# Block products of the up projection: weight sums made by accumulating transfers, and 17 block tiles instead of 12 in the first network

## The chip, the cores and the metric

One core of one Trainium2 chip runs the kernel. The metric is device time of one execution in microseconds (us), the median of several runs. The core has a matrix engine (PE; its weight loads are shown as PEld), a vector engine (VectorE, DVE in the profile), an activation engine (ScalarE, ACT), a general engine (GpSimd, POOL) and an engine that mostly issues transfers (SyncE, SP). Each engine works through a queue of its own in order, and waits on semaphores for what other engines or transfers have to finish first.

## The reference: what is computed

Two residual layers over 512 tokens of width 1024, everything in float32. Each layer has a token mixer (first a state-space mixer, "s5", then forgetting attention, "fox") and a gated feed-forward network with a short convolution. Only the networks are touched here:

```
def conv_ffn(h, w_up, conv_w, conv_b, w_down):
    up = h @ w_up                       # (512, 1024) @ (1024, 5632)
    a, b = jnp.split(up, 2, axis=-1)    # two branches of 2816 columns
    ...
    a_conv = conv_b
    for i in range(CONV_W):             # causal, width 3
        a_conv = a_conv + ap[:, i:i + S] * conv_w[i]
    return (jax.nn.silu(a_conv) * b) @ w_down
```

## The kernel before, in words

**Precision.** Every float32 matrix is split in two float32r parts, `hi` (a rounded copy, made by ScalarE, L287) and `lo` (the rest, value minus `hi`, made by VectorE, L288). A product of two matrices is three matrix multiplies: hi·hi, hi·lo and lo·hi. This splitting is `put_parts`, L285. Weights arrive as float32 in tiles called `raw` (three buffers, L191), are split into a ring of five `w_hi` tiles and five `w_lo` tiles (L272 to L283, L195), and only then reach PE.

**Stages.** `build` (L1504) runs s5, the first network (`ffn`, L597, with l = 0), fox, and the second network (l = 1). A network has 22 column tiles f of 128 columns in each branch. The weights of tile f are two `raw` tiles of 512 KB, number 2f for the convolved branch and 2f + 1 for the other. The 22 tiles are worked in four groups of 6, 5, 6 and 5 (`GROUPS`); while a later group is made, the down projection of the group before is worked off in pieces between its tiles (`down`, L672), 18 or 15 matrix multiplies of 512 columns for each of 8 output tiles. `gated` (L614) does convolution, silu, the product of the branches and the split of the result.

**Two ways to make a tile.** A tile in `WHOLE_TILES` (L49) goes through `product` (L308, with `apart=True`): two weight tiles, two halves of 256 tokens, 8 blocks of the inner dimension and three parts, so 96 matrix multiplies of 256 columns, from L304. Any other tile goes through `quarters` (L529), which treats the two weight tiles as a 2 by 2 block matrix (rows: a = tile 2f, b = tile 2f + 1; columns: the two halves of the inner dimension) and the tokens likewise, and forms the product with seven block products instead of eight, Winograd's form of Strassen's scheme: 7 × 4 × 3 = 84 matrix multiplies of 256 columns, from L566. It needs four sums of weight quarters, which VectorE makes in the tiles `sums` (L548, L549, L551, L552; they all go through the helper of L537 and carry its number in the profile):

- s1 = a21 + a22, s2 = s1 − a11, s3 = a11 − a21, s4 = a12 − s2

and four sums of the tokens, made once for each network by `forms_x` (L490). The quarters a11, a12, s1, s2, s4, s3 and a22 are then split in that order of writing; a22 goes into a tile of its own, `e`, with one buffer. PE takes them in the order a11, s1, a12, s2, s4, a22, s3 (L579 to L592), 12 matrix multiplies each. Three of the products pile up on others in PSUM: s2 on a11, s4 on s1, s3 on both of a11 and s2. In between ScalarE has to copy the earlier sum out (`copy`, L571 and L573), and VectorE adds the copies into the result (L584, L588, L593, L594).

**What sets the order.** The kernel is written for a framework that traces the program and, at build time, places each instruction in the queue of its engine by its place in the program and by when it expects operands and buffers to be ready; `issue_after` adds an order by hand. The queues are fixed when the kernel runs. The first network also works off the modulation vectors of later sub-layers in the background (`ada_units`, L248: one VectorE instruction on 128x1024 elements with a transfer of 512 KB; two for each tile from f = 6 on, `SUMS`, L50).

**Before the change** the first network makes tiles 0 to 4, 8, 11, 14, 17 and 20 whole and the other 12 by blocks; the second makes tiles 0 to 3 whole and 18 by blocks. No transfer is issued from GpSimd.

Of the kernel before, what the change touches and what calls it, by code (L numbers as in the profile page):

```python
# [45 lines left out]
ROWS_FROM = 0  # L46
GROUPS = (6, 5, 6, 5)
TAIL = 4
WHOLE_TILES = (0, 1, 2, 3, 4, 8, 11, 14, 17, 20), (0, 1, 2, 3)  # L49
SUMS = (0,) * 6 + (2,) * 16  # L50
FIRST = (("c", (KT,)), ("s5_prm", (3, G // 2)))
REST = (
# [11 lines left out]
class Trunk:  # L64
# [425 lines left out]
    def forms_x(self, pool, x, b):  # L490
# [10 lines left out]
                yield  # L501
        self.tx = {}

        def form(n, u, v):
            t = pool.tile([P, H, N], F32, name="sums", bufs=2)
            nc.vector.tensor_tensor(t, u, v, ALU.subtract)
# [12 lines left out]

        f1 = form(1, b[0][:, :, t2], b[0][:, :, t1])  # L520
        yield
        f2 = form(2, b[1][:, :, t2], f1)
        yield
        form(4, f2, b[1][:, :, t1])
        yield
        form(3, b[1][:, :, t2], b[0][:, :, t2])
        yield

    def quarters(self, pool, l, f, x, finish):  # L529

        nc = self.nc
        H, N = KT // 2, S // 2
        t1, t2 = HALVES
        a, b = (self.raw([P, KT, P], self.io["w_up"][l][2 * f + j]) for j in range(2))
        a11, a12, a21, a22 = a[:, :H], a[:, H:], b[:, :H], b[:, H:]
        c, d = (pool.tile([P, 2, H, P], F32, name="sums", bufs=2) for _ in range(2))
        sub = lambda o, u, v, op=ALU.subtract: nc.vector.tensor_tensor(o, u, v, op)  # L537
# [12 lines left out]
        parts(c.rearrange("p n k m -> p (n k) m"), ("s1", "s2"))  # L550
        sub(d[:, 1], a11, a21)  # L551
        sub(d[:, 0], a12, c[:, 1])  # L552
        parts(d.rearrange("p n k m -> p (n k) m"), ("s4", "s3"))
        e = self.e or [pool.tile([P, H, P], F32R, name=n, tag="e" + n, bufs=1) for n in ("w_hi", "w_lo")]
        self.e = None
        parts(a22, ("a22",), e)
        quarter = lambda k, t: tuple(v[:, k * H:(k + 1) * H, t] for v in x)
        xs = {"b11": quarter(0, t1), "b21": quarter(1, t1), "b22": quarter(1, t2)}
        for n, v in self.tx.items():
# [8 lines left out]
                        skip_group_check=True,  # L568
                    )

        def copy(o):  # L571
            t = self.tmp.tile([P, N], F32, name="nm_h", bufs=4)
            nc.scalar.activation(t, o, AF.Copy)  # L573
            return t

        p1, p5 = (self.mm.tile([P, S], F32, name="mmp")[:, :N] for _ in range(2))
# [14 lines left out]
        c4 = copy(p4)  # L591
# [104 lines left out]
class Ew:  # L696
# [29 lines left out]
    def sub(self, a, b, out=None):  # L726
        return self.tt(a, b, ALU.subtract, out)
# [875 lines left out]
```

## Time and profile before

| | |
|---|---|
| median of 3 runs | 1193.79 us (1190.88 to 1197.5) |
| the profiled execution | 1197.65 us, of which the span from first to last instruction is 1195.9 us |
| PE busy | 1174.1 us, 98% |
| VectorE busy | 988.7 us, 83% |
| ScalarE busy | 592.4 us, 50% |
| GpSimd busy | 62.6 us, 5% |
| granted TensorE clock, mean | 0.991 |
| block tiles of the first network, with the down projection between | from 310 to 564 us |
| block tiles of the second network, likewise | from 891 to 1148 us |

A row of the groups reads: line, engine, operation, output<-inputs, shape, count | busy us, mean ns of one | idle time of the engine just before them, and what ended it. In a timeline the columns are start in us, length in us, engine, line, operation, tiles, and in square brackets the idle time before it and what ended it; SPq is SyncE's queue that issues transfers, and its lengths include waiting for a free buffer. PE's matrix multiplies are pipelined: one lasts longer than the distance to the next, so their pace is read from the starts.

### The profile page before, as it was taken

How to read it: one execution, taken by the hardware profiler on the slowest of the kernel's cores; microseconds unless marked ns; L12 is line 12 of the kernel's file. 1: busy time of each engine (PE TensorE's matmuls, PEld its weight loads, DVE VectorE, ACT ScalarE, POOL GpSimd, SP SyncE). 2: the span in 40 equal slices, each digit the busy share in tenths (PEclk: the TensorE clock that was granted, in tenths of full speed). 3: DMA queues.
4: the chain of work that ended last, by engine and by line, in shares of the span. 5: the costliest groups of instructions: out<-in, count | busy, mean ns of one | idle time of the engine just before them, and what ended most of it. 6: DMA issues, size and time to landing. Idle time of an engine off the chain costs nothing.

```text
span 1195.9 us, 21116 instructions
## 1 busy us (share of the span) xinstructions
PE 1174.1 (98%) x8243; PEld 1026.5 (86%) x8243; DVE 988.7 (83%) x1824; ACT 592.4 (50%) x1069; POOL 62.6 (5%) x114
## 2 busy tenths in 40 slices
PE   7999999999999999999999999999999999999997
PEld 2455687899999999999899788878999999999987
DVE  8899977889888888887776788866899888888855
ACT  2554525346544454453453566554466555555543
POOL 1000000000000000000000443330000000000000
PEclk9999989999999999999999999999999999999999
DMA  9687758822264455554514655523123342343331
GB/s 359 226 256 251 230 167 303 295 92 89 87 204 131 159 174 170 185 184 139 194 36 138 209 185 166 200 76 97 47 75 96 124 124 86 111 124 95 104 88 72
DMA packets 73234, 183.83 MB, mean 154 GB/s; under 512 B 23231, under 2 KB 25503, under 8 KB 72111
## 3 DMA queue, kind: packets, MB, share of 16 engines
q1 hardware_dynamic: 72847, 181.96, 46.6%
q8 instruction: 65, 1.06, 0.4%
q10 hardware_dynamic: 288, 0.52, 0.1%
q14 instruction: 34, 0.28, 0.1%
HBM read 175.53 MB, written 6.92 MB: 153 GB/s over the span
## 4 chain that ended last, share of the span: by engine, by line
PE 86%; DVE 7%; DMA 3%; ACT 2%; issue 1%; POOL 0%; SPq 0%; DVEq 0%; ACTq 0%; POOLq 0%
PE mmp L304 42%; PE mmp L566 15%; PE aux L566 6%; PE mmp L1167 4%; PE mmp L1344 3%; PE mmp L1197 2%; DVE w_lo L288 2%; PE aux L1490 2%; PE aux L1473 1%; PE aux L1061 1%; PE aux L1053 1%; PE mmp L221 1%; PE aux L1443 1%; ACT w_hi L287 1%; DMA raw<-in_w_down 1%
## 5 line engine op out<-in xcount | busy, mean ns | idle before, releaser
L287 ACT ACTIVATE w_hi<-raw 128x1024 fp32r<-128x1024 f32 (+4 forms) x197 | 176.0, 900 | 146.9 <-PE mmp L304 75.5
L288 DVE TENSOR_TENSOR w_lo<-raw,w_hi 128x1024 fp32r<-128x1024 f32 (+4 forms) x197 | 203.4, 1036 | 29.7 <-ACT w_hi L287 25.2
L304 PE MATMUL mmp<-a_hi,w_hi 128*128 128x256 f32 (+1 forms) x600 | 185.9, 311 | 0.0
L304 PE MATMUL mmp<-a_hi,w_lo 128*128 128x256 f32 (+1 forms) x600 | 182.8, 306 | 0.0
L304 PE MATMUL mmp<-a_lo,w_hi 128*128 128x256 f32 (+1 forms) x600 | 182.7, 305 | 0.0
L304 PE MATMUL mmp<-ghi,w_hi 128*128 128x512 f32 (+1 forms) x392 | 143.9, 367 | 0.0
L304 PE MATMUL mmp<-glo,w_hi 128*128 128x512 f32 (+1 forms) x392 | 143.9, 367 | 0.0
L304 PE MATMUL mmp<-ghi,w_lo 128*128 128x512 f32 (+1 forms) x392 | 143.6, 366 | 0.0
L304 PEld LDWEIGHTS mmp<-a_hi,w_hi 128*128 128x128 f32 x600 | 112.4, 188 | 7.6 <-issue 2.6
L304 PEld LDWEIGHTS mmp<-a_hi,w_lo 128*128 128x128 f32 x600 | 112.5, 188 | 6.4
L304 PEld LDWEIGHTS mmp<-a_lo,w_hi 128*128 128x128 f32 x600 | 112.6, 188 | 4.8
L287 ACT ACTIVATE w_hi<-sums 128x1024 fp32r<-128x1024 f32 x68 | 71.6, 1060 | 65.9 <-DVE sums L537 27.4
L566 PE MATMUL mmp<-w_hi 128*128 128x256 f32 x360 | 99.6, 277 | 0.0
L566 PE MATMUL mmp<-w_hi,w_lo 128*128 128x256 f32 x360 | 99.5, 276 | 0.0
L566 PE MATMUL mmp<-w_lo,w_hi 128*128 128x256 f32 x360 | 99.4, 276 | 0.0
L288 DVE TENSOR_TENSOR w_lo<-sums,w_hi 128x1024 fp32r<-128x1024 f32 x68 | 82.4, 1220 | 7.6 <-ACT w_hi L287 6.5
L256 DVE CUSTOM_DVE_ANT_0 ada_raw<-ada_raw,ada_c,rest 128x1024 f32<-128x1024 f32 x64 | 83.7, 1326 | 5.1 <-DMA ada_raw<-in_ada_rows 5.1
L304 PEld LDWEIGHTS mmp<-ghi,w_lo 128*128 128x128 f32 x392 | 73.6, 188 | 12.3
L304 PEld LDWEIGHTS mmp<-ghi,w_hi 128*128 128x128 f32 x392 | 73.6, 188 | 11.2
L304 PEld LDWEIGHTS mmp<-glo,w_hi 128*128 128x128 f32 x392 | 73.6, 188 | 11.1
L378 DVE SCALAR_TENSOR_TENSOR h<-mmp,par,h 128x512 f32<-128x512 f32 (+1 forms) x98 | 62.9, 649 | 23.4 <-PE mmp L304 23.3
L566 PEld LDWEIGHTS mmp<-w_hi 128*128 128x128 f32 x360 | 67.6, 188 | 0.1
(317 smaller groups left out, 2833.0 us busy)
## 6 DMA issues: line engine op xcount, KB each, us to landing
raw<-in_w_up SPq DMA_DIRECT2D x88, 512.0 KB, 3.4
ada_raw<-in_ada_rows SPq DMA_DIRECT2D x64, 512.0 KB, 4.2
raw<-in_ada_w SPq DMA_DIRECT2D x32, 512.0 KB, 5.5
raw<-in_w_down SPq DMA_DIRECT2D x32, 384.0 KB, 3.2
raw<-in_w_down SPq DMA_DIRECT2D x32, 320.0 KB, 3.1
nf<-nfd SPq DMA_DIRECT2D x8, 1152.0 KB, 5.7
raw<-in_fox_qk SPq DMA_DIRECT2D x16, 512.0 KB, 3.2
h<-in_x SPq DMA_DIRECT2D x8, 512.0 KB, 5.5
```

The source lines that it names most:

```text
L221: self.last_mm = nc.tensor.matmul(ps[32 * qq:32 * qq + 32, :], self.sc32[:, k, :], w[:, q * S:(q + 1) * S], start=(step is steps[0]), stop ...
L256: nc.vector.tensor_tensor_reduce(w, w, self.crow, 1.0, self.ada_b[:, i, m:m + 1], ALU.mult, ALU.add, self.par[i][:, m:m + 1])
L287: nc.scalar.activation(hi, src, AF.Copy)
L288: self.late = (nc.vector.tensor_tensor(lo, src, hi.bitcast(F32), ALU.subtract).ins,)
L304: self.last_mm = self.nc.tensor.matmul(o, wt, xt[:, cols], start=(k == 0 and n == 0), stop=(k == nk - 1 and n == 2),)
L378: self.nc.vector.scalar_tensor_tensor(h, v, self.par[i][:, 16 + m:17 + m], h, op0=ALU.mult, op1=ALU.add,).ins,
L566: self.last_mm = nc.tensor.matmul(o, wt[:, k], xt[:, k], start=(first and k == 0 and n == 0), stop=(k == H - 1 and n == 2), skip_group_che ...
L1053: nc.tensor.matmul(yp[g2][:, k, :], t[:, 2 * k + g2], u[:, g, :], start=(k == 0), stop=False, skip_group_check=True,)
L1167: nc.tensor.matmul(ps, w[m][:, k, :], x[:, k], start=(k == 0), stop=(k == KT - 1))
L1197: nc.tensor.matmul(gps[m], wt, xt[:, k], start=(k == 0 and part == 0 and xt is yhi), stop=(k == KT - 1 and part == 1))
L1344: self.last_mm = nc.tensor.matmul(ps[q, b][:, :n], xt[:, k, tb], wt, start=(k == 0 and i == 0), stop=(k == KT - 1 and i == 2),)
L1490: nc.tensor.matmul(pv[:, c * P:], self.v[:, hp, k, r].rearrange("p t d -> p (t d)"), pp[:, r, c + 3 * k:NB + 3 * k, :].rearrange("p b t -> ...
```

## The change: sums by accumulating transfers, and fewer whole tiles

The four VectorE instructions for the weight sums are dropped. In their place come two ScalarE instructions that write negated copies, −a11 into a new tile `s2` (128x512, one buffer) and −a11, −a12 into `d` (128x1024, two buffers), and four transfers of 256 KB issued from GpSimd that add their source to what stands at the destination. `src` is the second weight tile in HBM:

1. a22 from HBM onto a21 in the raw tile `b`, which becomes s1;
2. a21 from HBM onto −a11 in `d`, which becomes −s3;
3. s1 from `b` onto −a11 in `s2`, which becomes s2;
4. s2 from `s2` onto −a12 in `d`, which becomes −s4.

The third needs the first, the fourth the third. The signs of t1, t3, s3 and s4 are turned, so that nothing else has to be negated but one copy out of PSUM. The split order is now (a11, a12), (s1, a22), (s2), (s3, s4), with s2 instead of a22 in the tile `e`. All this holds for all block tiles of both networks. In the first network tiles 8, 11, 14, 17 and 20 become block tiles.

```
-WHOLE_TILES = (0, 1, 2, 3, 4, 8, 11, 14, 17, 20), (0, 1, 2, 3)
+WHOLE_TILES = (0, 1, 2, 3, 4), (0, 1, 2, 3)
...
-        f1 = form(1, b[0][:, :, t2], b[0][:, :, t1])
+        f1 = form(1, b[0][:, :, t1], b[0][:, :, t2])
-        f2 = form(2, b[1][:, :, t2], f1)
+        f2 = form(2, b[1][:, :, t2], f1, ALU.add)
-        form(3, b[1][:, :, t2], b[0][:, :, t2])
+        form(3, b[0][:, :, t2], b[1][:, :, t2])
...
+        src = self.io["w_up"][l][2 * f + 1]
-        c, d = (pool.tile([P, 2, H, P], F32, name="sums", bufs=2) for _ in range(2))
+        d = pool.tile([P, 2, H, P], F32, name="sums", bufs=2)
+        s2 = pool.tile([P, H, P], F32, name="sum2", bufs=1)
+        plus = lambda o, u: nc.gpsimd.dma_start(o, u, accum_op=ALU.add)
...
+        plus(b[:, :H], src[:, H:])
+        nc.scalar.activation(s2, a[:, :H], AF.Copy, scale=-1.0)
+        nc.scalar.activation(d.rearrange("p n k m -> p (n k) m"), a, AF.Copy, scale=-1.0)
         parts(a, ("a11", "a12"))
-        sub(c[:, 0], a21, a22, ALU.add)
-        sub(c[:, 1], c[:, 0], a11)
-        parts(c.rearrange("p n k m -> p (n k) m"), ("s1", "s2"))
-        sub(d[:, 1], a11, a21)
-        sub(d[:, 0], a12, c[:, 1])
-        parts(d.rearrange("p n k m -> p (n k) m"), ("s4", "s3"))
+        plus(d[:, 0], src[:, :H])
+        plus(s2, b[:, :H])
+        parts(b, ("s1", "a22"))
+        plus(d[:, 1], s2)
         e = self.e or [pool.tile([P, H, P], F32R, name=n, tag="e" + n, bufs=1) for n in ("w_hi", "w_lo")]
-        parts(a22, ("a22",), e)
+        parts(s2, ("s2",), e)
+        parts(d.rearrange("p n k m -> p (n k) m"), ("s3", "s4"))
...
-        c5 = copy(p5)
+        c5 = copy(p5, -1.0)
...
-        sub(oa[:, t2], p5, c2, ALU.add)
+        sub(oa[:, t2], c2, p5)
```

More of the change, by code (lines that the diff above doesn't have):

```diff
@@ L502, in forms_x, with form @@
         self.tx = {}
-        def form(n, u, v):
+        def form(n, u, v, op=ALU.subtract):
             t = pool.tile([P, H, N], F32, name="sums", bufs=2)
-            nc.vector.tensor_tensor(t, u, v, ALU.subtract)
+            nc.vector.tensor_tensor(t, u, v, op)
             if n == 1:
@@ L533, in quarters @@
         t1, t2 = HALVES
+        src = self.io["w_up"][l][2 * f + 1]
         a, b = (self.raw([P, KT, P], self.io["w_up"][l][2 * f + j]) for j in range(2))
-        a11, a12, a21, a22 = a[:, :H], a[:, H:], b[:, :H], b[:, H:]
-        c, d = (pool.tile([P, 2, H, P], F32, name="sums", bufs=2) for _ in range(2))
+        d = pool.tile([P, 2, H, P], F32, name="sums", bufs=2)
+        s2 = pool.tile([P, H, P], F32, name="sum2", bufs=1)
         sub = lambda o, u, v, op=ALU.subtract: nc.vector.tensor_tensor(o, u, v, op)
+        plus = lambda o, u: nc.gpsimd.dma_start(o, u, accum_op=ALU.add)
         w = {}
@@ L569, in times, with copy @@
                     )
-        def copy(o):
+        def copy(o, scale=1.0):
             t = self.tmp.tile([P, N], F32, name="nm_h", bufs=4)
-            nc.scalar.activation(t, o, AF.Copy)
+            nc.scalar.activation(t, o, AF.Copy, scale=scale)
             return t
```

## The prediction

> **What bounds the kernel now.** I read the page's head first, then its chain of waits.
>
> ```profile
> span 1195.9 us, 21116 instructions
> PE 1174.1 (98%) x8243; PEld 1026.5 (86%) x8243; DVE 988.7 (83%) x1824; ACT 592.4 (50%) x1069; POOL 62.6 (5%) x114
> PE 86%; DVE 7%; DMA 3%; ACT 2%; issue 1%; POOL 0%; SPq 0%; DVEq 0%; ACTq 0%; POOLq 0%
> ```
>
> PE is both the busiest engine and 86% of the chain that ends last. An average hides stages, so the next view is the stretches in which block tiles are made: the first network, the first 44 us of block tiles in the second, and the rest of the second. The columns after the stretch are its length and each engine's busy time, then the granted clock, the DMA share and GB/s.
>
> ```profile
> 310.30:564.00 253.70, 253.70 (x1863) 238.99 (x1862) 216.20 (x320) 119.38 (x178) 0.52 (x1) 1.00 0.51 165
> 890.90:935.00 44.10, 43.81 (x360) 42.64 (x359) 42.55 (x64) 26.75 (x45) 0.00 (x0) 1.00 0.36 120
> 935.00:1148.40 213.40, 213.40 (x1528) 199.53 (x1527) 179.86 (x267) 113.75 (x177) 0.00 (x0) 1.00 0.35 107
> ```
>
> PE has no hole in the first and the third, and 0.3 us in the second, at full clock. VectorE is close behind: 85%, 96% and 84%. So in these stages time is gained only by giving PE fewer matrix multiplies, and lost wherever a weight or a freed PSUM bank comes later than PE asks for it. GpSimd does next to nothing there.
>
> **What the five exchanged tiles save.** The pace of PE is read from where a tile of each kind begins and where the work behind it begins: a whole tile first, then a block tile.
>
> ```profile
> 351.20 0.28 PE L304 MATMUL mmp<-a_hi,w_hi 128*128 128x256 f32 x1
> 362.11 0.39 PE L304 MATMUL mmp<-ghi,w_hi 128*128 128x512 f32 x1
> ...
> 366.21 0.28 PE L566 MATMUL mmp<-a_hi,w_hi 128*128 128x256 f32 x1
> 375.76 0.39 PE L304 MATMUL mmp<-ghi,w_hi 128*128 128x512 f32 x1
> ```
>
> A whole tile takes 362.11 − 351.20 = 10.91 us for 96 matrix multiplies, a block tile 375.76 − 366.21 = 9.55 us for 84; both go at 0.1137 us each, so neither waits for anything. The difference is 1.36 us, and five tiles make **6.8 us**. This is the whole gain in sight: the other 30 block tiles keep their 84 multiplies.
>
> **What moves between VectorE and ScalarE.** The groups by form give the prices.
>
> ```profile
> L288 DVE TENSOR_TENSOR w_lo<-raw,w_hi 128x1024 fp32r<-128x1024 f32 x100 | 123.8, 1242 | 21.6 <-ACT w_hi L287 17.2 <-PE aux L1344 3.7
> L288 DVE TENSOR_TENSOR w_lo<-sums,w_hi 128x1024 fp32r<-128x1024 f32 x68 | 82.4, 1220 | 7.6 <-ACT w_hi L287 6.5
> L287 ACT ACTIVATE w_hi<-sums 128x1024 fp32r<-128x1024 f32 x68 | 71.6, 1060 | 65.9 <-DVE sums L537 27.4 <-PE mmp L304 22.5 <-PE aux L566 5.7
> L537 DVE TENSOR_TENSOR sums<-raw 128x512 f32<-128x512 f32 x60 | 39.3, 687 | 20.9 <-DMA raw<-in_w_up 20.8
> L537 DVE TENSOR_TENSOR nm_t<-mmp,nm_h 128x256 f32<-128x256 f32 x90 | 35.3, 418 | 0.0
> L573 ACT ACTIVATE nm_h<-mmp 128x256 f32<-128x256 f32 x90 | 33.8, 377 | 42.1 <-PE mmp L566 42.1
> L288 DVE TENSOR_TENSOR w_lo<-raw,w_hi 128x512 fp32r<-128x512 f32 x30 | 20.5, 685 | 0.0
> L287 ACT ACTIVATE w_hi<-raw 128x512 fp32r<-128x512 f32 x30 | 18.7, 622 | 6.9 <-DMA raw<-in_w_up 6.8
> ```
>
> Each block tile loses four sums of 0.687 us on VectorE: 2.75 us, 33 us for the 12 old tiles of the first network and 49 us for the 18 of the second. Each exchanged tile gains on VectorE 3 × 1.22 + 0.685 − 2 × 1.242 = 1.86 us of splitting and four additions at 0.418, together 3.53 us, 17.7 us for five. VectorE in the first network goes from 216.2 to 216.2 − 33 + 17.7 = 201 us, of a stretch of 253.7 − 6.8 = 246.9, or 81%; in the second from 42.55 + 179.86 = 222.4 to 173 of 44.1 + 213.4 = 257.5, or 67%. As PE did not wait for VectorE before, none of this shortens anything; it is what makes room for the five tiles.
>
> ScalarE takes two negations a tile. No row shows one; the nearest are its copies of 128x512 and 128x1024, 0.622 + 1.060 = 1.68 us, and I take that. Over 17 tiles that is 28.6 us; the exchanged tiles add 5 × (3 × 1.060 + 0.622 − 2 × 1.06 + 4 × 0.377) = 16 us. ScalarE reaches 119.4 + 44.6 = 164 of 246.9 us, 66%, and about the same in the second network. Under PE's cover both cost nothing; the cover is gone only where an engine's order of work stands still, which is the rest of this text. The turned signs and the scaled copy keep their instructions and their prices.
>
> **What the transfers cost.** The trace has no transfer issued from GpSimd and none that adds. The nearest rows are other queues' transfers (size, then median us from issue to landing).
>
> ```profile
> raw<-in_w_up SPq DMA_DIRECT2D x88, 512.0 KB, 3.4
> nf<-nfd SPq DMA_DIRECT2D x8, 1152.0 KB, 5.7
> yt<-s_yd SPq DMA_DIRECT2D x16, 256.0 KB, 4.8
> s_ud<-uf SPq DMA_DIRECT2D x8, 256.0 KB, 3.1
> nfd<-nf_rows SPq DMA_DIRECT2D x1, 16.0 KB, 1.5
> ```
>
> The ends are 1.5 us (almost no bytes) and 5.7 us (over four times the bytes). The same size takes 3.1 and 4.8, and I take their middle, **4.0 us** each. The Trainium skill ("DMA: Bandwidth & Descriptors", the section on the anatomy of one SWDGE DMA) fits 2.0 us plus bytes over 436 GB/s to plain transfers issued by GpSimd, by which I estimate 2.6 us for 256 KB, and the three in a row would take 7.8 us; no run here shows one yet.
>
> Three of the four hang on each other (s1, then s2, then s4), so s4 is there three transfers after the second weight tile has landed, 12.0 us, and 1.06 + 1.22 = 2.28 us of splitting later PE can have it. PE wants it four products after the tile's begin, 48 × 0.1137 = 5.46 us. Two tiles of the second network show how much time there is: the line in which VectorE waits for the landing of the raw tile, and the tile's begin on PE.
>
> ```profile
> 945.98 1.29 DVE L537 TENSOR_TENSOR sums<-raw 128x512 f32<-128x512 f32 x2 [0.82 <-DMA raw<-in_w_up]
> 955.91 0.28 PE L566 MATMUL mmp<-a_hi,w_hi 128*128 128x256 f32 x1
> ...
> 977.26 1.30 DVE L537 TENSOR_TENSOR sums<-raw 128x512 f32<-128x512 f32 x2 [1.69 <-DMA raw<-in_w_up]
> 991.47 0.28 PE L566 MATMUL mmp<-a_hi,w_hi 128*128 128x256 f32 x1
> ```
>
> The first has 955.91 + 5.46 − 2.28 − 945.98 = 13.1 us for three transfers, the second 17.4. At 4.0 us each they fit with 1.1 and 5.4 us to spare; the chain is late in the first from 4.4 us a transfer on, in the second from 5.8. The shorter chains (s1 one transfer, s2 two) have more room. The raw buffers turn over differently too: the first weight tile is free as soon as ScalarE and VectorE have copied and split it, where it now waits for the last sum, and the second is held through two transfers. With three buffers I set this at nothing; if it goes wrong, it is a load that waits in SyncE's queue, with the loads of the down projection behind it.
>
> The 140 transfers of 256 KB add 1.05 MB a tile of about 14.5 us, 72 GB/s. By the rate of the first row of stretches (0.51 for 165 GB/s) that is 0.22 of the DMA time, or 0.45 if the destination's reading counts again: 0.73 to 0.96 in the first network, less in the second. It fits, barely at the upper end.
>
> **Sum.** The profiled execution took 1197.65 us, 1.75 more than its span and 3.86 more than the median. −6.8 for the five tiles, 0 for the rest: 1190.85 in its terms, and 1193.79 − 6.8 = **1187.0 us** in the terms of the median. Runs before spread over 6.6 us, so about 0.5% (6 us) is what a measurement here can tell from no change; the forecast lies just beyond it.
>
> **First rival: the dense stretch comes late.** At the beginning of the second network's block tiles there is no down projection between them and the lead is nothing now:
>
> ```profile
> 891.30 8.43 SPq L192 DMA_DIRECT2D raw<-in_w_up  x3
> ...
> 907.26 1.29 DVE L537 TENSOR_TENSOR sums<-raw 128x512 f32<-128x512 f32 x2
> 910.28 1.23 DVE L288 TENSOR_TENSOR w_lo<-sums,w_hi 128x1024 fp32r<-128x1024 f32 x1 [0.20 <-ACT w_hi L287]
> ...
> 911.38 0.28 PE L566 MATMUL mmp<-w_hi 128*128 128x256 f32 x1
> 911.61 0.34 PE L566 MATMUL mmp<-w_hi,w_lo 128*128 128x256 f32 x1
> ```
>
> The lo part of s1 is ready at 911.51, and PE uses it at 911.61, with a multiply stretched to 0.34 us. If the chain begins no earlier than the sums do now, s4 of this tile has 911.38 + 3 × 1.364 − 2.28 − 907.26 = 5.9 us for 12 us of transfers and is 6.1 us late. One such delay moves everything behind it, so it is paid about once: 1187 + 6 = 1193 us. Against it: the sums and the loads are late here because VectorE is 96% busy and holds the raw buffers (the three loads above waited 8.4 us in their queue); four tiles without sums take 11 us off those 42.55.
>
> **Second rival, slower: ScalarE stands before a transfer that has not landed, with a copy out of PSUM behind it.** Three of a tile's four splits now wait for an accumulating transfer. PE comes back to the bank of the first product after two others, 24 × 0.1137 = 2.73 us; the copy takes 0.38, so ScalarE may be stuck for 2.35 us before PE stops, and from there PE pays each microsecond. The queue's order was fixed at build time on an expected transfer time, and it decides how often this happens. If each of 35 tiles pays 1 us, it is 1187 + 35 = 1222 us. What the waits say:
>
> ```profile
> ACT w_hi L287 <- PE mmp L304: 98.0, 54, 4.5
> ...
> ACT w_hi L287 <- DMA raw<-in_w_up: 11.8, 10, 3.1
> ...
> PE mmp L566 <- ACT nm_h L573: 0.3, 1, 0.3
> ```
>
> (Columns: us in all, times, longest.) For it: ScalarE does stand before loads, up to 3.1 us. Against it: that cost PE 0.3 us once, and most splits wait for PE to free a buffer, 98 us in all, so their data has been there for some time.
>
> **Third rival: VectorE slows the issuing.** If each transfer's issue waits behind one VectorE instruction of about 1.22 us, a transfer takes 5.2 us and the chain 15.7: 2.6 us late in the tile of 955.91, in time in that of 991.47. Were half of 35 tiles late by that, it would be 45 us; a late tile leaves more time to the next, so I take a quarter, 11 us: 1198 us. The Trainium skill ("SBUF — State Buffer", the section on who interferes with whom) says that GpSimd shares a pair of SBUF ports with VectorE and that a transfer which GpSimd issues can starve behind VectorE in its two-port modes; it also infers that additions of two tensors, nearly all that runs here, do not block it. No run here shows either, and that keeps the chance low.
>
> That the change does not do what it says, I exclude for its gain: the number of matrix multiplies follows from the code.
>
> **How the numbers follow.** The forecast has 0.50 (own range 1184 to 1190), the first rival 0.22, the second 0.20, the third 0.08. Faster by over 0.5% means below 1187.8: 0.38 of the forecast's and 0.02 of the first rival's chance, together 0.40. Slower by over 0.5%: the second rival, 0.06 of the first and 0.05 of the third, 0.31. The rest is 0.29. The range begins at 1184, the forecast less 3 us of spread, and ends at 1214, which takes in the first and third rival and the second up to 0.8 us a tile; some 0.06 lie below and 0.12 above.
>
> **What would show it.** Right: PE's multiplies fall from 8243 by 60; the sums of L537 are gone; the stretch of the first network is about 247 us with no hole in PE, VectorE near 81%, ScalarE near 66%; the adding transfers land in about 4 us. Wrong: rows in which PE waits for ScalarE's copies (second rival), for a split behind a transfer in the first tiles of the second network (first) or in many tiles, with transfers beyond 4.4 us (third, if they are long in issuing rather than in moving). A chain below 4 us with PE waiting all the same would mean that the buffers, not the transfers, were misjudged.

## The result, and the profile after

The kernel with the change takes 1401.85 us, median of 4 runs (1397.11 to 1414.5), against 1193.59 us for the kernel before in 4 runs (1190.88 to 1197.5). The ratio is 1.1765, 95% interval 1.1726 to 1.1804: 208 us slower, far outside the range of the prediction. The profiled execution took 1401.83 us.

The head of its page:

```profile
span 1400.1 us, 21428 instructions
PE 1226.4 (88%) x8183; PEld 1064.8 (76%) x8183; DVE 938.0 (67%) x1734; ACT 646.7 (46%) x1169; POOL 185.1 (13%) x254
```

PE has 60 multiplies fewer, as the code says, but from 98% of the span it has fallen to 88%. No engine has become the bound: VectorE went from 83 to 67%, ScalarE from 50 to 46%. Something is waited for.

The stretches with block tiles: the first network, the first 44 us of block tiles in the second, and the rest (columns: stretch, length, busy time of PE, PEld, DVE, ACT, POOL, granted clock, DMA share, GB/s).

```profile
304.00:666.00 362.00, 280.69 (x1803) 258.03 (x1803) 208.85 (x307) 151.16 (x239) 54.56 (x64) 0.89 0.62 157
1000.90:1045.00 44.10, 33.15 (x238) 32.43 (x237) 25.73 (x35) 23.85 (x37) 11.44 (x13) 0.85 0.68 143
1045.00:1352.10 307.10, 252.25 (x1652) 232.32 (x1651) 159.38 (x227) 137.77 (x219) 49.96 (x57) 0.92 0.56 128
```

The first network takes 362 us where before it took 254, the second 351 where it took 258. These two differences are 202 of the 204 us between the profiled executions, so the cause lies in the stretches with block tiles. The clock has fallen to 0.85 to 0.92, from 1.00.

To split the loss I took the distance from each multiply's start to the next in these stretches and subtracted what it is at full pace (0.113 us for 256 columns, twice that for 512). A single excess above 0.15 us and above the multiply's own time counts as a standstill, a smaller one as slow pace:

```
             first network                   second network
             length  full pace  still  slow   length  full pace  still  slow
before       253.8   252.7       0.0    0.8   257.6   255.4       0.5    1.4
after        361.9   245.9      89.6   26.1   351.3   255.4      72.0   23.5
```

The full pace of the first network went from 252.7 to 245.9 us: it counts the multiplies at one fixed distance, so it shows that the 60 multiplies of the predicted 6.8 us are gone. 161.6 us of standstill and 49.6 us of slow pace bury them.

Who waits for whom (us in all, times, longest):

```profile
ACT w_hi L287 <- DMA sum<-raw: 186.7, 34, 12.1
ACT w_hi L287 <- DMA raw<-in_w_up: 77.2, 14, 10.3
ACT w_hi L287 <- DMA sums<-sum: 67.8, 29, 4.9
...
PE mmp L570 <- ACT nm_h L577: 122.4, 32, 11.1
...
SPq L192 <- DMA sum<-raw: 240.6, 35, 10.8
```

PE's wait for ScalarE's copies out of PSUM has grown from 0.3 us once to 122.4 us in 32 waits. ScalarE itself stands 332 us in its splits before accumulating transfers or loads: the third transfer (`sum<-raw`), the first one or a load (both are `raw<-in_w_up`), and the fourth (`sums<-sum`). In 14 of PE's waits, 86.9 us, it stands before the last product of a tile; nearly all others are before the fourth. The last row is of SyncE's queue and is new too: 35 loads, one for each block tile, wait for a third transfer that still reads the raw buffer. Waiting as such is not new to these loads: before, they waited 528.1 us for VectorE's splits and 115.4 us for its sums, and now it is 603.3 us for the splits beside the 240.6.

One such standstill in order of time, engine by engine:

```profile
419.26 15.70 SPq L192 DMA_DIRECT2D raw<-in_w_up  x2
...
439.22 0.87 POOL L539 DMA_DIRECT2D raw<-in_w_up  x1 [2.45 <-DVE h L378]
447.87 0.89 POOL L539 DMA_DIRECT2D sum<-raw  x1 [7.78 <-DMA raw<-in_w_up]
451.55 0.88 POOL L539 DMA_DIRECT2D sums<-sum  x1 [2.79 <-DMA sum<-raw]
...
433.39 1.22 DVE L288 TENSOR_TENSOR w_lo<-raw,w_hi 128x1024 fp32r<-128x1024 f32 x1
...
428.69 0.63 ACT L287 ACTIVATE w_hi<-sum 128x512 fp32r<-128x512 f32 x1 [10.47 <-DMA sum<-raw]
...
431.40 1.05 ACT L287 ACTIVATE w_hi<-raw 128x1024 fp32r<-128x1024 f32 x1
...
447.28 1.06 ACT L287 ACTIVATE w_hi<-raw 128x1024 fp32r<-128x1024 f32 x1 [9.15 <-DMA raw<-in_w_up]
451.23 0.63 ACT L287 ACTIVATE w_hi<-sum 128x512 fp32r<-128x512 f32 x1 [2.89 <-DMA sum<-raw]
451.77 0.37 ACT L577 ACTIVATE nm_h<-mmp 128x256 f32<-128x256 f32 x1
...
452.19 0.58 PE L570 MATMUL mmp<-w_hi 128*128 128x256 f32 x1 [9.89 <-ACT nm_h L577]
452.57 0.41 PE L570 MATMUL mmp<-w_lo,w_hi 128*128 128x256 f32 x1
452.78 0.41 PE L570 MATMUL mmp<-w_hi,w_lo 128*128 128x256 f32 x1
```

SyncE asks for the next tile's two loads at 419.26, but the second is out only 15.70 us later, since its buffer is held: until 428.69 the third transfer of the tile before reads it, and then the split of s1 and a22, which stands behind that of s2 in ScalarE's queue (431.40), is done on VectorE only at 434.61. So 9.1 us of this wait belong to the transfer and 5.8 us to the split. The first transfer of that tile is issued at 439.22 and has landed at 447.2, the third at 451.2. ScalarE waits for each in turn (9.15 and 2.89 us), and behind these two splits, which belong to the **next** tile, stands the copy at 451.77 that PE needs for the tile in hand. PE stands still for 9.89 us and then goes on at 0.21 us a multiply instead of 0.113.

The transfers themselves, from issue to landing (size, median us):

```profile
raw<-in_w_up SPq DMA_DIRECT2D x88, 512.0 KB, 3.9
...
raw<-in_w_up POOLq DMA_DIRECT2D x35, 256.0 KB, 5.8
sum<-raw POOLq DMA_DIRECT2D x35, 256.0 KB, 3.3
sums<-in_w_up POOLq DMA_DIRECT2D x35, 256.0 KB, 5.2
sums<-sum POOLq DMA_DIRECT2D x35, 256.0 KB, 4.5
```

5.8 + 3.3 + 4.5 = 13.6 us for the chain of three, where 12.0 were predicted. With what lies between them (the first is issued some 0.7 us after the second weight tile has landed, the third 0.7 us after the first has, the fourth 0.4 us after the third), the chain from that landing to s4 takes 13.2 us at best and 16.0 us in the median tile.

### The profile page after: what moved, and what is told of

Same layout as the page of the kernel before. It is cut to its first block, busy times and chain, and to the rows that moved or that the text cites. A ratio compares the mean times of both kernels' runs of the same rounds, so it can differ in the third digit from the quotient of the medians.

```text
span 1400.1 us, 21428 instructions
## 1 busy us (share of the span) xinstructions
PE 1226.4 (88%) x8183; PEld 1064.8 (76%) x8183; DVE 938.0 (67%) x1734; ACT 646.7 (46%) x1169; POOL 185.1 (13%) x254
## 5 line engine op out<-in xcount | busy, mean ns | idle before, releaser
L288 DVE TENSOR_TENSOR w_lo<-raw,w_hi 128x1024 fp32r<-128x1024 f32 (+3 forms) x197 | 220.0, 1120 | 92.1 <-ACT w_hi L287 88.0
L287 ACT ACTIVATE w_hi<-raw 128x1024 fp32r<-128x1024 f32 (+3 forms) x197 | 188.0, 962 | 171.8 <-DMA raw<-in_w_up 77.2
L570 PE MATMUL mmp<-w_hi 128*128 128x256 f32 x420 | 133.1, 317 | 141.2 <-ACT nm_h L577 122.4
L304 PE MATMUL mmp<-a_hi,w_hi 128*128 128x256 f32 (+1 forms) x440 | 141.8, 324 | 0.0
L304 PE MATMUL mmp<-a_hi,w_lo 128*128 128x256 f32 (+1 forms) x440 | 138.6, 316 | 0.0
L304 PE MATMUL mmp<-a_lo,w_hi 128*128 128x256 f32 (+1 forms) x440 | 138.3, 316 | 0.0
L570 PE MATMUL mmp<-w_hi,w_lo 128*128 128x256 f32 x420 | 129.6, 309 | 6.0 <-DVE w_lo L288 6.0
L570 PEld LDWEIGHTS mmp<-w_hi,w_lo 128*128 128x128 f32 x420 | 90.9, 216 | 8.4 <-DVE w_lo L288 8.4
L570 PEld LDWEIGHTS mmp<-w_lo,w_hi 128*128 128x128 f32 x420 | 90.7, 216 | 0.0
L304 PEld LDWEIGHTS mmp<-ghi,w_hi 128*128 128x128 f32 x392 | 78.0, 199 | 13.2 <-issue 1.2
L304 PEld LDWEIGHTS mmp<-a_hi,w_lo 128*128 128x128 f32 x440 | 82.4, 188 | 6.4
```

The costliest lines, as they stand in the source:

```text
L287: nc.scalar.activation(hi, src, AF.Copy)
L288: self.late = (nc.vector.tensor_tensor(lo, src, hi.bitcast(F32), ALU.subtract).ins,)
L304: self.last_mm = self.nc.tensor.matmul(o, wt, xt[:, cols], start=(k == 0 and n == 0), stop=(k == nk - 1 and n == 2),)
L570: self.last_mm = nc.tensor.matmul(o, wt[:, k], xt[:, k], start=(first and k == 0 and n == 0), stop=(k == H - 1 and n == 2), skip_group_che ...
```

## The experiments

Two theories. **Queue order**: the data would do, but ScalarE's queue was laid out for transfers that land sooner, so splits that nobody needs yet stand before copies that PE needs at once. **Late data**: the sums are there too late for PE however the queue is ordered, because of the chain, because the held raw buffer delays the loads, or because the transfers crowd out each other. All runs beside each other (us; the stretches by the accounting above; last column: PE's waits for the copies):

```
run                                           time    network 1  network 2  copies
before                                        1193.6    253.8      257.6      0.3
after                                         1401.9    361.9      351.3    122.4
e1_ord      splits behind the last copies     1385.2    359.8      344.4    135.0
e2_idle     before, with idle transfers       1210.9    259.9      271.4     13.2
e3_v17      before, with 17 block tiles       1210.5    263.1      258.3      2.2
e4_buf      own buffers for the second tile   1297.3    293.1      296.2     54.2
e5_buford   the two of e1 and e4              1311.9    309.1      300.2     62.8
e6_pool17   sums as additions on GpSimd       1284.1    299.6      302.0     65.5
e7_sbsrc    first transfer from SBUF          1392.5    350.4      351.0    111.1
e8_t12      12 block tiles, with transfers    1341.2    304.5      350.9     68.9
e9_c0       no transfer                       1187.8    248.4      256.5      0.7
e10_c1      transfers 1 and 2                 1224.8    269.7      267.8     21.4
e11_c2      transfers 1 to 3                  1339.0    329.5      322.4     93.4
e12_bfirst  second tile loaded first          1308.6    326.9      299.0     74.1
e13_hold    3 transfers, the third holds b    1312.9    322.3      310.5     82.5
e14_chain   3 transfers, the third depends    1320.4    328.8      309.6     88.3
e15_bfbuf   the two of e4 and e12             1293.5    293.8      296.8     55.3
e16_c0buf   e9 with the buffers of e4         1204.5    248.0      257.2      0.8
e17_holdord the two of e1 and e13             1275.1    297.8      288.0     36.0
e18_bford   the two of e1 and e12             1308.2    322.8      299.5     72.2
```

The kernel before took 1191.8 to 1196.0 us beside them. All experiments but e9 were timed once, and the four runs of the changed kernel spread over 17 us, so differences of that size and less between them carry nothing.

### Splits behind the copies, idle transfers, seventeen tiles, own buffers

e1 places the three splits that wait for transfers behind the last copy and the last addition of the tile before:

```
+        with self.behind(*self.ahead):
+            parts(b, ("s1", "a22"))
...
+            self.copied = nc.scalar.activation(t, o, AF.Copy, scale=scale).ins
...
+        last = sub(ob[:, t1], p1, c4).ins
+        self.ahead = (self.copied, last)
```

(and so for the splits of s2 and of s3, s4).

> The changed kernel, with one order added: the splits of s1 and a22, of s2 and of s3 and s4 are queued on ScalarE and VectorE behind the last copy and the last addition of the block tile before. Queue theory (ScalarE stands before a transfer that has not landed, with the copies out of PSUM behind it): PE's waits for these copies, 131 us, fall below 15 us, and the time falls from 1400 us to 1250 or less. Ring theory (the sums come late anyway, because the second weight tile is held through two transfers and the next load waits for its buffer): the waits for copies go, but PE waits for split weights instead, and the time stays at 1340 to 1400 us. Contention theory (the transfers slow other traffic and engines): 1380 to 1400 us.

```profile
PE mmp L572 <- ACT nm_h L579: 135.0, 26, 8.3
...
ACT w_hi L287 <- DMA sums<-sum: 118.3, 30, 6.5
ACT w_hi L287 <- DMA raw<-in_w_up: 73.7, 22, 5.2
ACT w_hi L287 <- DMA sum<-raw: 56.5, 24, 4.4
...
408.85 1.06 ACT L287 ACTIVATE w_hi<-sums 128x1024 fp32r<-128x1024 f32 x1 [4.26 <-DMA sums<-sum]
...
411.27 0.36 ACT L579 ACTIVATE nm_h<-mmp 128x256 f32<-128x256 f32 x1
...
411.69 0.58 PE L572 MATMUL mmp<-w_hi 128*128 128x256 f32 x1 [6.51 <-ACT nm_h L579]
```

Only some 16 us came back, no more than the spread of the changed kernel, and the waits for copies, which should have gone by both theories, are still there. They have moved: before the last product of a tile they fell from 86.9 to 1.6 us, before the fourth they rose from 35.6 to 133.3. ScalarE now stands before the tile's own transfers, with the tile's own copies behind them. The last three rows show one: the split of s3 and s4, which PE needs for its fifth product, stands before the copy that it needs for the fourth, and so it is in 24 of the 25 tiles that wait there. So e1 takes away the order between tiles and not the order within a tile. Late data are the rest: were the copies in time and the trace otherwise as it is, PE would still wait for s4 itself, by an estimate from the rows of these 24 tiles (the end of the split of s3 and s4, less the time at which PE would have come to s4) for some 54 of their 129 us.

e2 is the kernel before with four idle accumulating transfers of 256 KB for each of its 30 block tiles, for which nobody waits:

```
+        for i in (src[:, H:], src[:, :H], row, row):
+            nc.gpsimd.dma_start(self.idle, i, accum_op=ALU.add)
```

> The kernel before, with 12 block tiles and its sums on VectorE, and beside it four accumulating transfers of 256 KB for each block tile that add onto a tile of their own which nobody reads; the first two read HBM, the last two SBUF, and each waits for the one before. Queue and ring theory: nobody waits for them, so the time stays within 10 us of before (1185 to 1205 us). Contention theory: 1230 us or more. The landing of a transfer: 3 to 6 us in both.

```profile
raw<-in_w_up SPq DMA_DIRECT2D x88, 512.0 KB, 4.6
...
idle<-in_w_up POOLq DMA_DIRECT2D x60, 256.0 KB, 4.6
idle<-ada_c POOLq DMA_DIRECT2D x60, 256.0 KB, 3.7
```

18 us slower than the kernel before on the same chip (1192.39), 0.6 us a tile, between the two expectations. The loads of weights take 4.6 instead of 3.4 us. The crowding that the prediction priced at nothing has a price, though a tenth of the loss.

e3 is the kernel before with `WHOLE_TILES` of the change and the sums left on VectorE.

> The kernel before with nothing changed but the 17 block tiles in the first network; sums on VectorE, no transfer that adds. All theories of the loss: no loss like that of the changed kernel. PE has 6.8 us less to do; VectorE has 216.2 + 5 x 6.28 = 247.6 us of work in a stretch that should shrink to 246.9, so some of the gain is lost: 1185 to 1200 us.

```profile
310.00:573.00 263.00, 253.67 (x1786) 236.21 (x1786) 238.85 (x368) 130.50 (x206) 0.52 (x1) 0.99 0.49 158
```

VectorE is at 238.85 of 263 us, 91%, and the kernel loses 18 us on the one before, 9 of them in this stretch. So with the sums on VectorE five more block tiles gain nothing.

e4 loads the second weight tile into buffers of its own, so that holding it delays only the next but one; the room comes from one `raw` and one `ada_raw` buffer.

```
-RAW, WB = 3, 5
+RAW, WB = 2, 5
...
+        b = pool.tile([P, KT, P], F32, name="braw", bufs=2)
+        nc.sync.dma_start(b, src)
```

> The changed kernel with the second weight tile of a block tile in two buffers of its own; paid for with two instead of three common raw buffers and one instead of two for the background's rows, so the first network and the stages outside the networks are not comparable, and the stretch of block tiles in the second network is read (257.5 us before, 351 us changed; nothing runs in the background there). Ring theory: that stretch falls below 285 us. Queue theory: it stays above 320 us, since the order is still fixed on a short transfer and ScalarE still stands before the sums with the copies behind it.

Half of the loss is gone: 1297 us, with 54.2 us of waits for copies left; the second stretch, 296 us, lies between the two expectations. The held raw buffer is one of the causes, and no small one.

### Order and buffers together, additions on GpSimd, source and number

e5 joins the edits of e1 and e4.

> The changed kernel with both edits: the second weight tile in two buffers of its own (paid for as in the run before with these buffers) and the splits of the transferred sums queued behind the copies and additions of the block tile before. In the second network's stretch (257.5 us before, 351 changed, 296 with the buffers alone): if what is left is the order of the queues, it falls below 275 us; if it is the lateness of the sums themselves, it stays at 290 us or more.

1312 us, no better than e4 alone. With these buffers the hand-made order brings nothing. But again the waits stand before the fourth product, 55.7 of 62.8 us behind the tile's own split of s3 and s4; by the estimate of e1 only some 6 us of them are s4's own lateness.

e6 drops the transfers: GpSimd makes the four sums of the kernel before with additions (`nc.gpsimd.tensor_tensor` in place of VectorE's), 17 block tiles.

> The kernel before with 17 block tiles and the four weight sums as additions on GpSimd instead of VectorE: no transfer that adds, no negation, the old signs. A sum of 128x512 on GpSimd took 1.48 us in the trace of before, so s4 is there about 4.5 us after the landing, where three transfers need 13. If the loss comes from the time between landing and last sum (ring theory), it is nearly gone: 1186 to 1200 us. If 17 block tiles are too many for any way of summing, or GpSimd and VectorE hinder each other: 1210 us or more.

```profile
PE mmp L567 <- ACT nm_h L574: 65.5, 26, 7.9
...
ACT w_hi L287 <- POOL sums L538: 125.9, 48, 6.5
...
SPq L192 <- POOL sums L538: 114.1, 35, 7.1
...
L288 DVE TENSOR_TENSOR w_lo<-raw,w_hi 128x1024 fp32r<-128x1024 f32 x95 | 138.1, 1456 | 27.7 <-ACT w_hi L287 23.2 <-PE aux L1345 3.7
```

An addition takes GpSimd 1.5 to 1.7 us where VectorE takes 0.69. Four of them, with no transfer at all, cost 96 us against e9, and the first three rows are those of the change: loads held, splits waiting, copies behind them. Accumulating transfers are thus only one way to be late; a slower maker of the sums, 6.6 us for all four, can do it too. Not all of the 96 us need be lateness, though: beside GpSimd's additions VectorE's splits take 1.46 us where they took 1.24, and no run tells what that costs.

e7 takes the source of the first transfer from SBUF, where the same quarter already lies: `plus(b[:, :H], b[:, H:])`.

> The changed kernel with one transfer changed: the first takes a22 from the raw tile in SBUF instead of from HBM again. In the changed kernel the transfers with an SBUF source land in 3.3 and 4.5 us, this one in 5.8. Ring theory: the time in which the second weight tile is held falls by about 2 us a tile, and as each tile's load waits for it, the kernel gains 1.5 to 2.5 us for most of 35 tiles: 1310 to 1350 us. Queue theory (order fixed on too short a transfer): a similar gain, as the wait itself is shorter. Contention theory (transfers crowd each other whatever their source): 1380 to 1405 us.

```profile
raw<-raw POOLq DMA_DIRECT2D x35, 256.0 KB, 5.8
```

5.8 us, as from HBM, and 1392 us: the length of the first transfer does not come from HBM. That idea fell, and as the transfer did not get shorter, the run says nothing on the theories.

e8 is the change with `WHOLE_TILES` of before.

> The transfers alone: the changed kernel with the old 12 block tiles in the first network. The second network stays as in the changed kernel (351 us for its stretch). Ring and queue theory: a whole tile gives the chain time to catch up, so the first network's loss against before falls from 115 us to 40 to 80, and the time is 1330 to 1365 us. If the loss is a fixed price for each block tile (4.9 us of waits, 5.9 with the slower pace): 1400 - 5 x 5.9 + 6.8 = 1377 us.

1341 us. The second network, the same in both, keeps its 351 us. The loss belongs to the transfers, about 5 us for each of 30 tiles, and the five exchanged tiles add to it. It is no fixed price for a tile: 12 block tiles lose 51 us in the first network, 17 lose 108.

### Fewer transfers, and the second tile first

e9, e10 and e11 remove transfers from the change: all four, the third and fourth, the fourth alone. The negations, the splits and 17 tiles stay.

```
-        plus(b[:, :H], src[:, H:])
...
-        plus(d[:, 0], src[:, :H])
-        plus(s2, b[:, :H])
...
-        plus(d[:, 1], s2)
```

> The changed kernel without its four transfers: the splits take the quarters and their negated copies as they are, so s1 to s4 are left out of the computation; 17 block tiles, ScalarE's negations and all splits remain. If the forecast's other terms hold (five tiles 6.8 us less for PE, negations and splits under cover): 1184 to 1192 us, a stretch of the second network of 255 to 259 us, no waits for copies. If ScalarE or the longer hold of a raw tile cost something by themselves: 1200 us or more.

> The changed kernel with the first and the second transfer alone, so that s2 and s4 are left out (negated quarters are split in their place); no transfer waits for another. Time-to-last-sum theory (what counts is the time from a raw tile's landing to its release and the last sum): about 6.5 us of chain, as with the sums on GpSimd, whose second stretch was 302 us: 290 to 305 us, the whole 1270 to 1300 us. If only the chain of three on the queues hurts: below 275 us and 1225 us.

> The changed kernel without the fourth transfer, so that s4 is left out: a chain of two. Time-to-last-sum theory: about 10 us of chain and the second raw tile held as long as in the changed kernel, so most of the loss remains: a second stretch of 325 to 350 us, the whole 1340 to 1395 us. If the fourth transfer, last in the chain, sets the pace: below 310 us.

The two networks of e9:

```profile
304.60:553.00 248.40, 247.71 (x1803) 232.59 (x1802) 206.30 (x305) 152.28 (x238) 0.52 (x1) 1.00 0.50 165
880.00:1136.50 256.50, 256.50 (x1887) 241.79 (x1886) 183.18 (x258) 162.99 (x253) 0.00 (x0) 1.00 0.34 105
```

Without transfers the change takes 1187.8 us, median of 10 runs, against 1191.77 in 13 of the kernel before: ratio 0.9967, interval 0.9948 to 0.9986. So the prediction's other terms hold: the first network has 248.4 us (246.9 forecast), VectorE is at 83%, and ScalarE's negations cost no time that shows. It also says what the change could gain at best: 4 us (1.7 to 6.2 by the interval), with the sums for nothing. The transfers then cost step by step 37 us (two independent ones), 114 us (the third on the first), 63 us (the fourth on the third). e10 missed what was expected of it: its two transfers, of which none waits for another, cost 37 us and not the 80 to 110 that its first expectation gives. So the time from landing to last sum alone does not set the loss; e11 lies at the lower edge of its range.

e12 loads the second weight tile, on which the first transfer waits, before the first one:

```
-        a, b = (self.raw([P, KT, P], self.io["w_up"][l][2 * f + j]) for j in range(2))
+        b, a = (self.raw([P, KT, P], self.io["w_up"][l][2 * f + j]) for j in (1, 0))
```

> The changed kernel with the order of the two raw tiles of a block tile turned: the second, with which the chain of transfers begins, is loaded first. In the changed kernel its load waits for a buffer until the third transfer of the tile before has landed, mostly over 10 us after the load of the first. Ring theory: the chain begins up to one transfer and one load earlier, and 4 to 8 us a tile of the block tiles that wait come back: 1250 to 1340 us. Queue theory: as the first tile's negations come later instead and the order is planned anew, little changes: 1370 us or more.

```profile
PE mmp L570 <- ACT nm_h L577: 74.1, 37, 6.2
...
SPq L192 <- DMA sum<-raw: 56.4, 25, 4.8
```

93 of the 208 us come back from exchanging two loads. The loads' waits for the third transfer fall from 240.6 to 56.4 us. Whether this is the same cause as in e4, approached from the other side, e15 tests.

### Holding or depending, and both remedies at once

The third transfer does two things: it depends on the first, and it holds `b`. e13 and e14 leave one of each (both without the fourth):

```
-        plus(s2, b[:, :H])
+        plus(s2, b[:, H:])
```

and for e14 `plus(s2, d[:, 0])`, behind the second transfer.

> Three transfers as in the run without the fourth (1339 us, second stretch 322 us), but the third reads the other half of the second raw tile, which the first does not write: so it still holds that tile, and no longer waits for the first transfer. s2 and s4 are left out of the computation. If the dependence on the first transfer (s2 late, ScalarE standing before it) costs: back near the run with two transfers, 1225 to 1260 us. If holding the raw tile costs: 1310 us or more.

> Three transfers again, but the third reads the tile of the second one (d) instead of the raw tile: so it waits for a transfer, as before, and no longer holds the raw tile. s2 and s4 are left out of the computation. If the hold of the raw tile costs: 1225 to 1260 us. If the dependence costs: 1310 us or more. Both in between: each has a share.

1313 and 1320 us, and with both properties (e11) 1339, where two transfers (e10) took 1225. Either alone costs most of it; they are not told apart, except that their costs don't add. A third property, which both runs keep and e10 lacks, would fit as well: s2's split waits for a transfer at all. ScalarE stands 105.1 us before it in e13 and 115.1 in e14. What e13 shows is how little the data need to be late:

```profile
1059.39 0.86 POOL L539 DMA_DIRECT2D raw<-in_w_up  x1 [2.81 <-DVE w_lo L288]
1059.95 1.20 POOL L539 DMA_DIRECT2D sum<-raw  x1
...
1067.34 0.63 ACT L287 ACTIVATE w_hi<-sum 128x512 fp32r<-128x512 f32 x1 [5.11 <-DMA sum<-raw]
1067.88 0.37 ACT L576 ACTIVATE nm_h<-mmp 128x256 f32<-128x256 f32 x1
...
1068.30 0.39 PE L569 MATMUL mmp<-w_hi 128*128 128x256 f32 x1 [2.97 <-ACT nm_h L576]
...
1079.54 0.28 PE L569 MATMUL mmp<-a_hi,w_hi 128*128 128x256 f32 x1
```

The third transfer lands 7 us after its issue, 12 us before PE begins the tile that uses it, at 1079.54. Nothing is late here, and yet PE stands for 2.97 us: the split that waits was placed before a copy of the tile in hand. That is queue order alone.

e15 joins e4 and e12, e16 is e9 with e4's buffers (a control).

> The changed kernel, whole computation, with the second weight tile loaded first and in two buffers of its own (paid for as in the run with these buffers). Second network's stretch, 296 us with the buffers alone and 299 with the order of the loads alone: if both remove the same wait (the chain's late begin), it stays at 285 to 300; if they remove different ones, it falls below 280. The crowding of the transfers alone, as in the run where nobody waits for them, would leave 271.

> Control for the runs with own buffers: the changed kernel without its four transfers (s1 to s4 left out of the computation) and with the buffers as there. If the payment (two common raw buffers, one buffer for the background's rows) costs nothing in the second network's stretch: 255 to 259 us there; what it costs elsewhere shows in the whole time, against 1188 us without that payment.

e15 brings nothing beyond e4 (1293.5, second stretch 297), as expected if both remove the same wait. e16 shows that e4's buffers by themselves cost some 17 us, all outside the block tiles, so in the networks e4 and e15 have undone more than their times say: by the table 124 of 202 us in e4.

### The order again, where no chain makes the data late

e17 is e13 with e1's order, e18 is e12 with it.

> The run with three transfers of which none waits for another (1313 us, second stretch 310 us; there ScalarE stands at the split of s2 for the next tile, which PE needs 16 us later, while a copy out of PSUM of the present tile waits behind it), with the splits of transferred sums queued behind the copies and additions of the block tile before. s2 and s4 are left out of the computation. Queue theory: the waits for copies, 83 us, fall below 20 and the second stretch to 280 us or less, the whole to 1250 or less. If the data are late anyway: 300 us and more.

> The changed kernel, whole computation, with both cheap edits: the second raw tile loaded first (1309 us alone, second stretch 299) and the splits queued behind the copies of the tile before (1385 us alone, 344). If the load order removes the lateness and what is left is the order on ScalarE: a second stretch below 280 us and 1255 us or less. If the chain of three stays late: 295 us or more and about 1300.

```profile
PE mmp L571 <- ACT nm_h L578: 36.0, 16, 6.0
...
SPq L192 <- DMA sum<-raw: 221.5, 33, 11.0
```

In e17 the waits for copies fall from e13's 82.5 to 36.0 us and the time from 1312.9 to 1275.1: where no chain makes the data late, the order is worth 38 us, of 125 over e9. 1275 us and a second stretch of 288 lie between the two expectations. The loads' waits for the third transfer rise meanwhile, from 109.5 us in e13 to 221.5, so these waits are by themselves no price. In e18, which has the whole chain, the order brings nothing (1308.2 against 1308.6). As in e1, its waits have moved before the fourth product: 64.0 of 72.2 us stand behind the tile's own split of s3 and s4, and by the estimate of e1 only some 10 us of them are s4's own lateness.

So both theories are part of the cause. That the transfers cause the loss is shown by e9. Removing lateness brings back about half, from two sides (e4, e12), and e6 loses 96 us with the same rows and no transfer; order is shown by e13 and e17, and in e1, e5 and e18 a part of it stays, the order within a tile, which no run removes. Open stays how much each has in the 208 us: data that come earlier are also less often missing where the queue stands, each edit lets the framework lay out the queues anew, and the estimates for e1, e5 and e18 leave out that a PE that waits less comes to the next tile earlier. Open is also why e4, e12, e15 and e18 all keep some 40 us of loss in the second network. No version of the whole computation was found that beats the kernel before, and e9 bounds what one could gain by hiding these transfers.

## Why the prediction was wrong

**The five tiles, −6.8 us: right.** The 60 multiplies are gone, and e9 has most of it in its time: its first network takes 5.4 us less than before. **Sums off VectorE, work onto ScalarE, both under PE's cover: right**, by e9's 83% of VectorE; and e3, 263.1 us for the stretch that takes e9 248.4, shows that the relief was needed.

**The chain of three, 12.0 us: too short.** The transfers' medians make 13.6, and the steps between them, which the sum left out, and transfers longer than the median bring the way from the landing to s4 to 16.0 us in the median. By the budgets of the prediction, 13.1 and 17.4 us for the tiles it looked at, that is late in one of them and in time in the other. From the fit of the Trainium skill ("DMA: Bandwidth & Descriptors", the section on the anatomy of one SWDGE DMA) for plain transfers the prediction estimated 2.6 us for 256 KB; the accumulating transfers here took 3.3 to 5.8 us in the median.

**"With three buffers I set this at nothing": the step that failed, with the chain.** The budgets took the landings of the second weight tile from the trace of before and left them there. But that tile is now held through two transfers, and through a split that stands behind another in ScalarE's queue, and the next tile's load waits for its buffer: 15.70 us in the rows shown, and 240.6 us for the transfers over 35 loads. So the chain not only takes longer, it begins later, and one tile's delay is handed to the next. The prediction named the sign of it, a load waiting in SyncE's queue, and e4 and e12, two ways of removing it, bring back some 100 us each.

**The second rival: the right mechanism, at less than a third of its price, with a chance of 0.20.** It put ScalarE before transfers that have not landed, with copies behind, at 1 us a tile. Over 35 tiles PE's waits for copies were 3.5 us a tile, all standstill was 4.6 and the slow pace 1.4. The argument against it, that most splits in before waited for PE and so their data had been there for long, was read from a kernel whose sums came at once. And the budgets asked when PE needs s4; the queue asks when ScalarE comes to the split, which is earlier: in e13 at 1062.23, 17 us before PE began the tile.

**The slow pace was not in the sum at all.** Behind a standstill PE goes at half clock:

```profile
452.20:456.40 4.20, 4.20 (x16) 3.91 (x17) 2.22 (x4) 0.81 (x1) 0.85 (x2) 0.50 0.81 189
```

Granted clock 0.50 for 4 us, after 9.89 us of waiting. The Trainium skill ("TensorE: Matmul & The Clock Gate", Part 1) says that PE falls to half clock after an idle window of about 3.4 us and needs as much busy time to come back; the trace agrees on the way back, 4.2 us here at 0.213 us a multiply in place of 0.113. Shorter waits were enough, though: after the 2.65 us that ended at 470.18 in the same trace and the 2.97 us shown of e13 half clock followed, in e13 1.3 us after PE had gone on, and lasted over 3 us. The 35 tiles lost 49.6 us by slow pace, about a quarter of the whole.

**Crowding, set at nothing: 18 us** in e2, where nobody waits for the transfers. **The third rival was not tested:** its chain of 15.7 us lies near the 16.0 measured, but with its cause not shown that counts as luck; an issue takes GpSimd 0.87 to 0.89 us in the rows shown, and no run tells whether VectorE delays what follows it. **The first rival**, late in the first tiles only, was too small a picture: PE waits for copies 32 times, through both networks.

## What to carry to other kernels

Before work is moved from an engine into a chain of transfers, follow the buffers that the chain holds: the next load, not the present product, may be what it delays. For each instruction that will wait for a transfer, ask what stands behind it on its in-order queue, and price the wait from the moment the engine gets there, not from the moment the data are needed. And make the run without the moved work first: here it showed that the best case was 4 us, less than the crowding alone.

## What the runs showed of the hardware

An accumulating transfer of 256 KB landed 3.3 to 5.8 us after its issue, by the medians of the four kinds. The first of a tile was as slow from SBUF as from HBM (5.8 us both, e7); in e2, where each waits for the one before, it was 3.7 us from SBUF and 4.6 from HBM. Four of them a tile lengthened the loads beside them from 3.4 to 4.6 us (e2). A standstill of 9.89 us was followed by 4.2 us at half clock, so it cost PE another 2.1 us. Beside additions on GpSimd VectorE's splits of 128x1024 took 1.46 us instead of 1.24 (e6).
